# A hybrid encoder layer on one core: six 2048x2048 products as Strassen-Winograd block products, with the weights as the moving operand

## The chip, the cores and the metric

The kernel runs on one core of a Trainium2 chip. The metric is the device time of one launch in microseconds (us); lower is better. Five engines take part, each with its own queue of instructions that starts them strictly in order: TensorE (PE: matmuls and transposes; its weight loads are listed apart as PEld), VectorE (DVE), ScalarE (ACT), GpSimd (POOL) and SyncE (SP), which here only issues DMAs; ScalarE issues some too. Instructions of different engines wait for each other by semaphores.

## The reference

One layer on 512 tokens of 2048 channels, in float32:

```python
h = rmsnorm(x, norm_w)
u = h @ w_in
z_ssm, xbc, dt_f, dt_b, q_a, kv_a, z_attn, g_ssm, g_attn = jnp.split(u, cuts, axis=-1)
# branch A: depthwise conv + SiLU on xbc, bidirectional chunked SSD scan, D skip
y = y.reshape(b, s, D_SSM) * jax.nn.silu(z_ssm)
y = rmsnorm(y.reshape(b, s, SSM_GROUPS, D_SSM // SSM_GROUPS),
            ssm_norm_w.reshape(SSM_GROUPS, D_SSM // SSM_GROUPS)).reshape(b, s, D_SSM)
# branch B: low-rank q and kv with RMSNorm, rotary part, softmax attention over 16 heads: o
o = o * jax.nn.silu(z_attn)
# merge: sigmoid gates, one projection per branch, output projection, residual
m = sigmoid(g_ssm) * (y @ w_proj_ssm) + sigmoid(g_attn) * (o @ w_proj_attn)
x = x + m @ w_out
```

and a last RMSNorm over the channels. Six of the products are 512x2048 by 2048x2048: the columns of w_in for z_ssm, g_ssm and g_attn, then w_proj_ssm, w_proj_attn and w_out. The scan works in four chunks of 128 tokens and four groups of eight heads.

## The kernel before, in words

Every float32 product is made from three matmuls in a rounded format: an operand is split into a high part (a cast on ScalarE) and a low part (the difference, on VectorE), and high x high, high x low and low x high are added up in PSUM (mm3, L158 to L160). Weights are stationary (128x128), 512 tokens are moving, and results have channels on the partitions ("dims-major"). A tile is 128 output channels: 16 blocks of the 2048 inputs by 3 matmuls, 48 in all. wchunk (L148 to L154) brings half a tile's weights, 128x1024: a load into the tile wraw, the cast to wh, the difference to wl, three buffers of each.

The activations h live in SBUF as h_h and h_l. The program runs: RMSNorm and transposes; the tile of dt; four scan groups; the rest of the gate tiles, the compressed q and kv; attention head by head; w_proj_ssm, w_proj_attn, w_out; final norm.

A scan group first computes its six tiles of xbc (conv and SiLU on ScalarE and VectorE) and then does the scan, a long chain of small steps over VectorE, ScalarE and GpSimd. While that chain runs, TensorE gets other tiles as fill: the group's four z tiles and eleven gate tiles. fill.run hands out their matmuls in 18 gaps, 40 in each, at fixed places of the program. A step (one chunk, half the group's heads) holds the making of a 128x512 decay matrix G (L548 to L559), a gap, and diag (L569 to L579), which multiplies G with the inputs, transposes the skip term yo (L575), adds and multiplies by z. The tile framework sets each engine's order from the order of the program, in which loads and splits of weights are moved ahead by a number of instructions (tc.high_priority).

The same way attention has fill from the next heads and, in its last head, from w_proj_ssm. The tag st names three buffers of 128x512 that all gate results and fetches share.

## Time and profile before

| | |
|---|---|
| median of three runs | 2069.2 us (2068.72 to 2069.51) |
| profiled execution | 2069.04 us |
| its span, first to last instruction | 2067.3 us |
| PE busy | 2035.6 us, 9498 instructions |
| VectorE, ScalarE, GpSimd busy | 1122.7, 791.2, 189.8 us |
| DMA | 252.16 MB, 122 GB/s in the mean |
| granted TensorE clock, mean | 0.998 |

A row of the groups reads: line, engine, operation, output<-inputs, shapes, number of instructions, busy us, mean ns of one, idle time of that engine before them and what ended it. A row of the DMA issues reads: destination<-source, queue, count, KB each, median us from issue to landing. A row of a timeline reads: start us, duration us, engine, line, operation. A row of windows reads: stretch, its length, then for PE, PEld, DVE, ACT and POOL the busy us with the number of instructions, then granted clock (1 is full), share of the DMA engines, GB/s.

### The profile page before, as it was taken

Reading aid. Unit: us, or ns where it says so; the run is one execution under the profiler, and the core shown is the slowest. Engines: PE = TensorE matmul, PEld = TensorE weight load, DVE = VectorE, ACT = ScalarE, POOL = GpSimd, SP = SyncE. Lnnn points to the kernel's source line nnn. Section 1 sums busy time; section 2 is a strip of 40 time slices with the busy share of each in tenths; the row PEclk is TensorE's granted clock in tenths of the full one; section 3 lists DMA queues with packets and bytes.
Section 4 is the critical chain, followed back from the end, with each engine's and each line's share of the span. In section 5 each row is a group of like instructions: output and inputs, shape, how many; then the busy total and the mean of one; then the engine's idle time right before and its main releaser. Section 6 shows DMA issues by size and latency. Waiting matters only on the chain.

```text
span 2067.3 us, 24135 instructions
## 1 busy us (share of the span) xinstructions
PE 2035.6 (98%) x9498; PEld 1681.3 (81%) x9498; DVE 1122.7 (54%) x1531; ACT 791.2 (38%) x1103; POOL 189.8 (9%) x139
## 2 busy tenths in 40 slices
PE   6999999999999999999999999999999999999998
PEld 5888888888888888888788888888878888888886
DVE  4646755567545675447674657677663334343342
ACT  5433443334433354334433434444442222222232
POOL 1031000311003100111100000000011010000110
PEclk9999999999999999999999999999999999999999
DMA  5423443245332453224433333323345444335342
GB/s 186 124 82 116 155 131 112 87 128 162 121 108 83 148 153 122 92 90 150 138 122 103 105 119 88 102 81 98 102 123 168 145 150 134 122 119 182 104 141 81
DMA packets 116881, 252.16 MB, mean 122 GB/s; under 512 B 11168, under 2 KB 44064, under 8 KB 116768
## 3 DMA queue, kind: packets, MB, share of 16 engines
q1 hardware_dynamic: 101088, 222.33, 34.7%
q10 hardware_dynamic: 15680, 28.29, 3.7%
q8 instruction: 74, 1.21, 0.2%
q14 instruction: 39, 0.32, 0.0%
HBM read 220.96 MB, written 25.43 MB: 119 GB/s over the span
## 4 chain that ended last, share of the span: by engine, by line
PE 98%; DVE 1%; DMA 1%; ACT 0%; issue 0%; ACTq 0%
PE gp L158 8%; PE gp L159 8%; PE gp L160 8%; PE mm L160 6%; PE mm L158 6%; PE mm L159 6%; PE zp L158 3%; PE zp L160 3%; PE f L997 3%; PE zp L159 3%; PE f L998 3%; PE f L999 3%; PE pb L845 1%; PE qp L160 1%; PE qp L158 1%; PE qp L159 1%
## 5 line engine op out<-in xcount | busy, mean ns | idle before, releaser
L154 DVE TENSOR_TENSOR wl<-wraw,wh 128x1024 fp32r<-128x1024 f32 (+2 forms) x332 | 401.7, 1210 | 571.5 <-ACT wh L153 549.2
L153 ACT CAST wh<-wraw 128x1024 fp32r<-128x1024 f32 (+1 forms) x336 | 341.3, 1017 | 828.8 <-PE gp L159 214.1
L158 PE MATMUL gp<-h_h,wh 128*128 128x512 f32 x768 | 302.4, 394 | 0.0
L159 PE MATMUL gp<-h_l,wh 128*128 128x512 f32 x768 | 299.2, 390 | 0.0
L160 PE MATMUL gp<-h_h,wl 128*128 128x512 f32 x768 | 299.1, 390 | 0.0
L158 PE MATMUL mm<-h_h,wh 128*128 128x512 f32 x544 | 215.2, 396 | 0.0
L160 PE MATMUL mm<-h_h,wl 128*128 128x512 f32 x544 | 212.0, 390 | 0.0
L159 PE MATMUL mm<-h_l,wh 128*128 128x512 f32 x544 | 211.8, 389 | 0.0
L160 PEld LDWEIGHTS gp<-h_h,wl 128*128 128x128 f32 x768 | 144.2, 188 | 30.3
L158 PEld LDWEIGHTS gp<-h_h,wh 128*128 128x128 f32 x768 | 144.3, 188 | 29.9 <-issue 0.9
L159 PEld LDWEIGHTS gp<-h_l,wh 128*128 128x128 f32 x768 | 144.3, 188 | 29.3 <-issue 0.2
L159 PEld LDWEIGHTS mm<-h_l,wh 128*128 128x128 f32 x544 | 102.2, 188 | 22.0 <-issue 1.2
L158 PEld LDWEIGHTS mm<-h_h,wh 128*128 128x128 f32 x544 | 102.2, 188 | 21.8 <-issue 1.2
L160 PEld LDWEIGHTS mm<-h_h,wl 128*128 128x128 f32 x544 | 102.1, 188 | 21.5
L158 PE MATMUL zp<-h_h,wh 128*128 128x512 f32 x256 | 100.5, 392 | 0.0
L160 PE MATMUL zp<-h_h,wl 128*128 128x512 f32 x256 | 99.7, 389 | 0.0
L159 PE MATMUL zp<-h_l,wh 128*128 128x512 f32 x256 | 99.6, 389 | 0.0
L548 DVE TENSOR_TENSOR_SCAN sum<-da,scn 128x512 f32<-128x512 f32 x64 | 83.4, 1318 | 0.0
L997 PE MATMUL f<-wh,mh 128*128 128x512 f32 x208 | 80.9, 389 | 0.0
L998 PE MATMUL f<-wl,mh 128*128 128x512 f32 x208 | 80.9, 389 | 0.0
L999 PE MATMUL f<-wh,ml 128*128 128x512 f32 x208 | 80.9, 389 | 0.0
L835 ACT ACTIVATE pr<-s,nm 128x512 f32<-128x512 f32 x64 | 44.1, 689 | 79.7 <-DVE nm L833 78.2
(3625 smaller groups left out, 3715.0 us busy)
## 6 DMA issues: line engine op xcount, KB each, us to landing
wraw<-wi SPq DMA_DIRECT2D x198, 512.0 KB, 3.5
da<-da_d SPq DMA_DIRECT2D x64, 256.0 KB, 3.8
wraw<-wps SPq DMA_DIRECT2D x32, 512.0 KB, 3.5
wraw<-wpa SPq DMA_DIRECT2D x32, 512.0 KB, 3.7
wraw<-wo SPq DMA_DIRECT2D x32, 512.0 KB, 3.5
wraw<-wun SPq DMA_DIRECT2D x16, 384.0 KB, 3.0
xt<-x SPq DMA_DIRECT2D x8, 512.0 KB, 8.5
zs_d<-gate ACTq DMA_DIRECT2D x16, 256.0 KB, 2.9
```

Of the source, the lines that this page charges most:

```text
L153: act.copy(h, raw)
L154: (dve if ahead[0] else pool).tensor_sub(l, raw, h.bitcast(F32))
L158: pe.matmul(out, wh, xh, start=start, stop=False)
L159: pe.matmul(out, wh, xl, start=False, stop=False)
L160: pe.matmul(out, wl, xh, start=False, stop=stop)
L548: dve.tensor_tensor_scan(sums[dd], flat(da), mask, 0.0, ALU.add, ALU.mult)
L835: act.activation(pr, s, AF.Exp, bias=nm, scale=SCALE, accum_out=sm_)
L845: pe.transpose(tp[:, k * P:(k + 1) * P], prs[t][:, k * P:(k + 1) * P], ident)
L997: pe.matmul(acc, mh[:, tk], h[k], start=(kk == 0), stop=False)
L998: pe.matmul(acc, mh[:, tk], l[k], start=False, stop=False)
L999: pe.matmul(acc, ml[:, tk], h[k], start=False, stop=(kk == KT - 1))
```

## The change

**The products.** The six 2048x2048 products are taken out of the scan, of attention and of the old tail, and all run behind attention, in the order wz, wgs, wga, wps, wpa, wo, each as a stage of the class Winograd. A stage splits the weights into 2x2 blocks in each of two column pairs cp, and the activations into 2x2 blocks (inputs by tokens). Of a pair it makes seven block products P1 to P7 (Winograd's form of Strassen) instead of eight, each of 48 matmuls: 14 x 48 = 672 in a stage, before 16 x 48 = 768. Weights (128x512) are now the moving operand, and a 128x128 piece of the activations is stationary, so results have tokens on the partitions.

**Operands.** A stage needs seven activation operands: the blocks x11, x12, x22 and the sums S1 to S4. x_op makes one in two halves from pieces of 512 KB read from DRAM: pieces go into buffers of the tag wraw (three, shared with the weights), are added up by GpSimd and VectorE, cast and split. The weight combinations are made by w_sub on GpSimd from the loads called held (eight buffers); the first combination, t3, is made in a wraw buffer. The three stages with input h share their operands. Each of wps, wpa and wo gets its own, made while the stage before runs its second pair (pass_on, make); for wo, whose input m is the result of wpa, S3 and x11 are made early from what is there, S1, S2 and x22 after wpa's last result, S4 and x12 after the transposes of that last result.

**Ways through DRAM.** h is added up from h_h and h_l again after scan group 0 (16 GpSimd additions hf, L633) and written out. The scan writes y unnormed, token-major (diag no longer transposes yo); norm and gate follow behind wz (done_z). Results that feed a product (y behind wz, m behind wpa) are transposed on TensorE (turn) and written out.

**The scan's fill.** The six xbc tiles of the next group and the ten tiles of the compressed q and kv are now fill, with the gate tiles of attention (za): 10, 10, 10 and 11 tiles, 26.7 matmuls in a gap (29.3 in the last group).

The core of the diff:

```diff
+    def qkv_gen(i, sq, new):
+        p_ = mm("qkv")
+        yield from gemm_steps(p_, win(T_QKV + i), h_h, h_l)
+        g_ = st("qkv")
+        act.copy(g_, p_)
+        put(qkv_d[i], g_)
+        if i in (0, 6):
+            act.activation(sq, p_, AF.Square)
+        else:
+            s2 = new("s2")
+            act.activation(s2, p_, AF.Square)
+            dve.tensor_add(sq, sq, s2)
...
+        if g + 1 < GROUPS:
+            for i in range(6):
+                fill.add(("xbc", g + 1) if i == 5 else "xbc", xbc_gen(g + 1, i))
+        for kind, n in ((("qkv", 4),), (("qkv", 4),), (("qkv", 2), ("za", 2)), (("za", 11),))[g]:
+            add_fill(kind, n)
+        left = [(10 * 48, 10 * 48, 10 * 48, 11 * 48)[g], 18]
...
-                yt = pb("yt")
-                for ct in range(4):
-                    pe.transpose(yt[:, ct * P:(ct + 1) * P], yo[:, c, ct * P:(ct + 1) * P], ident)
-                ys_ = tmp2("ys_")
-                act.copy(ys_, yt)
-                dve.tensor_add(ys_, ys_, yb)
-                dve.tensor_mul(zs[:, :, cs], zs[:, :, cs], ys_.rearrange("p (t l) -> p t l", t=4))
+                yt = st("yt")
+                dve.tensor_add(yt, yo[:, c], yb)
+                put(y_d[c][g], yt)
...
+        if g == 0:
+            for k in range(KT):
+                hf = st("hf")
+                pool.tensor_add(hf, h_h[:, k, :].bitcast(F32), h_l[:, k, :].bitcast(F32))
+                put(k_tile(h_d, k), hf)
+        if g == 2:
+            put(rkv_d, r_sum(sq_kv, KL, tmp2))
+        if g == 1:
...
+    def x_op(which, src, place):
+        op_pool, tag, n = place
+        op = op_pool.tile([P, 2, 8, 256], F32R, tag=tag, bufs=n, name=which)
+        for q in range(2):
+            def piece(ij):
+                t = wp.tile([P, 1024], F32, tag="wraw", bufs=3, name="xraw")
+                i, j = int(ij[0]) - 1, int(ij[1]) - 1
+                s_ = src[j].rearrange("p (k t) -> p k t", k=8)[:, 4 * q:4 * q + 4, i * 256:(i + 1) * 256]
+                nc.sync.dma_start(t.rearrange("p (k t) -> p k t", k=4), s_)
+                return t
+            def add(t, u):
+                pool.tensor_add(t, t, u)
+            def sub(t, u):
+                pool.tensor_sub(t, t, u)
+            def dadd(t, u):
+                dve.tensor_add(t, t, u)
+            def dsub(t, u):
+                dve.tensor_sub(t, t, u)
+            first, *rest = {"x11": ["11"], "x12": ["12"], "x22": ["22"], "S1": ["21", (add, "22")],
+                            "S2": ["21", (add, "22"), (dsub, "11")], "S3": ["11", (sub, "21")],
+                            "S4": ["12", (dadd, "11"), (dsub, "21"), (sub, "22")]}[which]
+            t = piece(first)
+            for f, ij in rest:
+                f(t, piece(ij))
+            t = t.rearrange("p (k t) -> p k t", k=4)
+            ks = slice(4 * q, 4 * q + 4)
+            act.copy(op[:, 0, ks], t)
+            dve.tensor_sub(op[:, 1, ks], t, op[:, 0, ks].bitcast(F32))
+        return op
...
+    def w_raw(w, cp, kh, cb, m, held=False):
+        with tc.high_priority(offset=LOAD_AHEAD if held else AHEAD):
+            if held:
+                t = xb.tile([P, 1024], F32, tag="held", bufs=8, name="held")
+            else:
+                t = wp.tile([P, 1024], F32, tag="wraw", bufs=3, name="wraw")
+            nc.sync.dma_start(t, a[w][cp, kh, cb, m])
+        return t
+    def w_sub(out, x, y):
+        with tc.high_priority(offset=AHEAD):
+            pool.tensor_sub(out, x, y)
+    def w_split(raw):
+        with tc.high_priority(offset=AHEAD):
+            h = wp.tile([P, 1024], F32R, tag="wh", bufs=3, name="wh")
+            l = wp.tile([P, 1024], F32R, tag="wl", bufs=3, name="wl")
+            act.copy(h, raw)
+            dve.tensor_sub(l, raw, h.bitcast(F32))
         return h, l
...
+    def rows(bank, op, i, m, w):
+        h, l = w
+        for jj in range(2):
+            j = 2 * m + jj
+            xh, xl = (op[:, s, j, i * P:(i + 1) * P] for s in range(2))
+            wh, wl = (t[:, jj * 512:(jj + 1) * 512] for t in (h, l))
+            pe.matmul(bank, xh, wh, start=(j == 0), stop=False)
+            pe.matmul(bank, xh, wl, start=False, stop=False)
+            pe.matmul(bank, xl, wh, start=False, stop=(j == 7))
+    def product(where, name, op, chunk):
+        banks = [b(name) for b in BANKS[where][name]]
+        for m in range(4):
+            w = w_split(chunk(m))
+            for i in range(2):
+                rows(banks[i], op, i, m, w)
+            yield 12
+        product_done()
+        yield banks
...
+        def t1(self, cp, m):
+            b11 = w_raw(self.w, cp, 0, 0, m)
+            w_sub(self.t[m], self.t[m], b11)
+            return b11
+        def t3(self, cp, m):
+            self.hold(cp, m)
+            t3 = wp.tile([P, 1024], F32, tag="wraw", bufs=3, name="t3")
+            w_sub(t3, self.b22[m], self.t[m])
+            return t3
...
+                yield from steps(product("head", "P7", self.op("S3"), lambda m: self.t3(0, m)), got)
+                self.p7 = evict(got.pop())
+                self.make(*ORDER)
+                yield from steps(product("head", "P1", self.op("x11"), lambda m: self.t1(0, m)), got)
...
+        def pair(self, cp):
+            w, got = self.w, []
+            end = cp == 1
+            if not end:
+                p7, p1 = self.p7, self.p1
+            else:
+                p1 = self.p1b
+                self.b22, self.t = [], []
+                def c7(m):
+                    t3 = self.t3(1, m)
+                    self.t1(1, m)
+                    return t3
+                yield from steps(product(1, "P7", self.op("S3"), c7), got)
+                p7 = evict(got.pop())
+                self.used("S3", "x11")
+            b22, t = self.b22, self.t
+            yield from steps(product(cp, "P5", self.op("S1"), lambda m: t[m]), got)
+            p5 = got.pop()
+            if end:
+                self.used("S1")
+                if self.nxt:
+                    self.nxt.make("S3", "x11")
+            def c6(m):
+                w_sub(t[m], b22[m], t[m])
+                return t[m]
+            yield from steps(product(cp, "P6", self.op("S2"), c6), got)
+            if end:
+                self.used("S2")
+                self.pass_on("S1")
+            p6 = got.pop()
+            us, vs_ = [], []
+            for i in range(2):
+                u = kp_.tile([P, SEQ], F32, tag="kk", bufs=2, name="u")
+                dve.tensor_add(u, p1[i], p6[i])
+                v = p7[i]
+                dve.tensor_add(v, v, u)
+                o22 = st("o22")
+                dve.tensor_add(o22, v, p5[i])
+                dve.tensor_add(u, u, p5[i])
+                us.append(u)
+                vs_.append(v)
+                self.done(2 + i, 2 * cp + 1, o22)
+            yield from steps(product(cp, "P3", self.op("S4"), lambda m: b22[m]), got)
+            if end:
+                self.used("S4")
+                self.pass_on("S2")
+            p3 = got.pop()
+            for i in range(2):
+                dve.tensor_add(us[i], us[i], p3[i])
+                self.done(i, 2 * cp + 1, us[i])
+            b21 = []
+            def c4(m):
+                b21.append(w_raw(w, cp, 1, 0, m, True))
+                w_sub(t[m], b21[m], t[m])
+                return t[m]
+            yield from steps(product(cp, "P4", self.op("x22"), c4), got)
+            if end:
+                self.used("x22")
+                self.pass_on("S4")
+            p4 = got.pop()
+            for i in range(2):
+                dve.tensor_add(vs_[i], vs_[i], p4[i])
+                self.done(2 + i, 2 * cp, vs_[i])
+            if end and self.w == "wo":
+                yield from self.last_product(p1, b21)
+                return
+            yield from steps(product(cp, "P2", self.op("x12"), lambda m: b21[m]), got)
+            if end:
+                self.used("x12")
+                self.pass_on("x22", "x12")
+                if self.nxt:
+                    self.nxt.make("S1", "S2", "x22")
+            p2 = got.pop()
+            for i in range(2):
+                dve.tensor_add(p1[i], p1[i], p2[i])
+                self.done(i, 2 * cp, p1[i])
...
+        def pass_on(self, *which):
+            if self.nxt and self.w != "wpa":
+                self.nxt.make(*which)
...
+    def turn(tile_, t, b, dst, n):
+        def f():
+            tp = pb("turn")
+            for i in range(4):
+                pe.transpose(tp[:, i * P:(i + 1) * P], tile_[:, i * P:(i + 1) * P], ident)
+            o = st("turned")
+            act.copy(o, tp)
+            d = dst[b // 2].rearrange("p (k t) -> p k t", k=8)[:, 4 * (b % 2):4 * (b % 2) + 4, t * P:(t + 1) * P]
+            act.dma_start(d, o.rearrange("p (k t) -> p k t", k=4))
+        after(n, f)
...
+    def done_z(t, b, z):
+        act.activation(z, z, AF.Silu)
+        y = fetch(y_d[t][b], "y")
+        dve.tensor_mul(z, z, y)
+        s_ = ssz[:, 4 * t + b:4 * t + b + 1]
+        act.activation(y, z, AF.Square, accum_out=s_)
+        dve.tensor_scalar(s_, s_, 1.0 / 512, EPS, ALU.mult, ALU.add)
+        r = rsqrt1(s_)
+        w = fetch(a["snw"][:, b * 512:(b + 1) * 512].broadcast_to([P, SEQ]), "snw")
+        dve.scalar_tensor_tensor(z, z, r, w, ALU.mult, ALU.mult)
+        turn(z, t, b, yn_d, 2)
...
+    def done_pa(t, b, o):
+        g_ = fetch(ga_d[t][b], "ga")
+        dve.tensor_mul(o, o, g_)
+        m_ = fetch(ms_d[t][b], "ms")
+        dve.tensor_add(o, o, m_)
+        turn(o, t, b, m_d, 1)
...
+    stages = [("wz", h_d, done_z), ("wgs", h_d, done_gate(gs_d)), ("wga", h_d, done_gate(ga_d)),
+              ("wps", yn_d, done_ps), ("wpa", o_d, done_pa), ("wo", m_d, done_o)]
+    prods = [Winograd(*s_) for s_ in stages]
+    for p_, q_ in zip(prods, prods[1:]):
+        if q_.src is p_.src:
+            q_.ops = p_.ops
+        else:
+            p_.nxt = q_
```

How the order moves, at three places. GpSimd, from the last decay matrices of scan group 0 into group 1 (G is the backward half of the decay matrix, c_l a split, yo the skip term and its sums, xw the weighted inputs from which the chunk states, loc, are made). Before:

```order
L557 TENSOR_TENSOR G_2036<-dtT,cbb 128x512
L557 TENSOR_TENSOR G_2124<-dtT,cbb 128x512
L447 TENSOR_TENSOR c_l<-CT,c_h 128x512
L483 TENSOR_TENSOR xw<-xT,wst 128x512 x2
L516 TENSOR_TENSOR yo<-xT,dsk 128x512 x4
```

Now:

```order
L599 TENSOR_TENSOR G_1904<-dtT,cbb 128x512
L633 TENSOR_TENSOR hf<-h_h,h_l 128x512 x13
L558 TENSOR_TENSOR yo<-xT,dsk 128x512
L633 TENSOR_TENSOR hf<-h_h,h_l 128x512
L558 TENSOR_TENSOR yo<-xT,dsk 128x512
L633 TENSOR_TENSOR hf<-h_h,h_l 128x512
L558 TENSOR_TENSOR yo<-xT,dsk 128x512 x2
L633 TENSOR_TENSOR hf<-h_h,h_l 128x512
L525 TENSOR_TENSOR xw<-xT,wst 128x512 x4
```

The sixteen hf stand between group 0's last G and group 1's first xw.

GpSimd, at the start of wz behind attention (held_9360, 9367, 9374 and 9381 take the weight combinations of the four chunks; xraw_9387 and 9394 become the two halves of S1, which P5 needs). Before, GpSimd had, towards the end of attention, only splits of y:

```order
L867 TENSOR_TENSOR y0l<-y0st,y0h 128x512
L867 TENSOR_TENSOR y2l<-y2st,y2h 128x512
L867 TENSOR_TENSOR y4l<-y4st,y4h 128x512
L867 TENSOR_TENSOR y6l<-y6st,y6h 128x512
L867 TENSOR_TENSOR y8l<-y8st,y8h 128x512
```

Now:

```order
L930 TENSOR_TENSOR held_9360<-held_9360,wraw_9362 128x1024
L930 TENSOR_TENSOR held_9367<-held_9367,wraw_9369 128x1024
L930 TENSOR_TENSOR held_9360<-held_9358,held_9360 128x1024
L930 TENSOR_TENSOR held_9374<-held_9374,wraw_9376 128x1024
L930 TENSOR_TENSOR held_9367<-held_9365,held_9367 128x1024
L930 TENSOR_TENSOR held_9374<-held_9372,held_9374 128x1024
L930 TENSOR_TENSOR held_9381<-held_9381,wraw_9383 128x1024
L884 TENSOR_TENSOR xraw_9387<-xraw_9387,xraw_9389 128x1024
L884 TENSOR_TENSOR xraw_9394<-xraw_9394,xraw_9396 128x1024
```

Seven weight subtractions stand ahead of the two additions of S1; three of them already belong to P6. On SP's queue, held_9381 stands ahead of the pieces of S1.

GpSimd, from the last product of wpa into wo (held_15021 to 15096 are weights of wpa's P4; xraw_15610 and 15617 become S1 of wo, 15625 and 15635 S2, 15779 and 15792 S4; t3 are the weights of P7). Before, GpSimd had no instruction between the last split of o and the tail. Now:

```order
L930 TENSOR_TENSOR held_15071<-held_15459,held_15071 128x1024
L930 TENSOR_TENSOR held_15096<-held_15478,held_15096 128x1024
L884 TENSOR_TENSOR xraw_15610<-xraw_15610,xraw_15612 128x1024
L884 TENSOR_TENSOR xraw_15617<-xraw_15617,xraw_15619 128x1024
L884 TENSOR_TENSOR xraw_15625<-xraw_15625,xraw_15627 128x1024
L884 TENSOR_TENSOR xraw_15635<-xraw_15635,xraw_15637 128x1024
L930 TENSOR_TENSOR t3_15674<-held_15670,held_15672 128x1024
L930 TENSOR_TENSOR t3_15696<-held_15692,held_15694 128x1024
L930 TENSOR_TENSOR t3_15718<-held_15714,held_15716 128x1024
L930 TENSOR_TENSOR t3_15740<-held_15736,held_15738 128x1024
L887 TENSOR_TENSOR xraw_15779<-xraw_15779,xraw_15787 128x1024
L887 TENSOR_TENSOR xraw_15792<-xraw_15792,xraw_15800 128x1024
```

S1 and S2 stand ahead of t3, S4 ahead of the weights of the second product. On SP's queue the pieces of S4 and x12 stand in the same way ahead of wraw_15816, the first weights of P1.

517 lines of the change are left out of this document (249 added, 268 removed).

## The prediction

> **What bounds the kernel now.** I read the page first: busy shares, slices, chain.
>
> ```profile
> span 2067.3 us, 24135 instructions
> PE 2035.6 (98%) x9498; PEld 1681.3 (81%) x9498; DVE 1122.7 (54%) x1531; ACT 791.2 (38%) x1103; POOL 189.8 (9%) x139
> PE   6999999999999999999999999999999999999998
> DVE  4646755567545675447674657677663334343342
> PE 98%; DVE 1%; DMA 1%; ACT 0%; issue 0%; ACTq 0%
> ```
>
> TensorE is busy in nearly every slice, and the chain that ended last is 98% TensorE work. VectorE has half its time free, GpSimd nine tenths. So removed matmuls pay in full, as long as nothing else becomes late; every microsecond in which TensorE waits is lost.
>
> Matmul records overlap (390 ns each), so their price is their distance, from the timeline of TensorE in the first projection, which runs at full clock:
>
> ```profile
> 1699.69 0.39 PE L159 MATMUL ps__13311<-y1l,wh 128*128 128x512 f32 x1
> ...
> 1702.41 0.39 PE L159 MATMUL ps__13311<-y5l,wh 128*128 128x512 f32 x1
> ```
>
> Twelve steps in 2.72 us: 0.2267 us a matmul, 10.88 us for a tile or block product of 48.
>
> **Prices of everything else**, from the groups by form, the DMA issues and the life of the tile wraw:
>
> ```profile
> L154 DVE TENSOR_TENSOR wl<-wraw,wh 128x1024 fp32r<-128x1024 f32 x292 | 367.8, 1260 | 556.3 <-ACT wh L153 535.2 <-PE rp L318 16.8 <-PE pb L298 4.2
> L153 ACT CAST wh<-wraw 128x1024 fp32r<-128x1024 f32 x296 | 311.2, 1052 | 787.2 <-PE gp L159 209.3 <-PE mm L159 178.0 <-PE f L999 68.9
> L154 POOL TENSOR_TENSOR wl<-wraw,wh 128x1024 fp32r<-128x1024 f32 x4 | 9.5, 2389 | 32.0 <-ACT wh L153 32.0
> L512 POOL TENSOR_TENSOR yo<-yo,tmp 128x512 f32<-128x512 f32 x24 | 36.9, 1552 | 184.3 <-DVE tmp L511 184.3
> L575 PE MATMUL yt<-cst,yo 128*128 128x128 f32 x64 | 10.5, 287 | 0.0
> wraw<-wps SPq DMA_DIRECT2D x32, 512.0 KB, 3.5
> y_d<-yn ACTq DMA_DIRECT2D x16, 256.0 KB, 2.0
> o_d<-og ACTq DMA_DIRECT2D x16, 256.0 KB, 3.7
> zs_d<-gate ACTq DMA_DIRECT2D x16, 256.0 KB, 2.9
> L150 SPq DMA_DIRECT2D wraw<-wps x32: 327/332/510, 1477.0 to 1680.9; - x32
> DMA to landing us min/median/max: 2.5/3.5/9.8
> ```
>
> On 128x1024, a VectorE subtraction is 1.26 us, a ScalarE cast 1.05, a GpSimd addition 2.39 (four operations only, the weakest row here); a GpSimd addition on 128x512 is 1.55; a 512 KB load lands in 3.5, a 256 KB store in 2.0 to 3.7. The new operand pieces have 1 KB runs instead of 4 KB, which no row shows; between 2.5 (the shortest landing) and 9.8 I take the median, since the size is that of the weight chunks. SP issues a load in 0.33 us; it gets about 800 instead of 574, and at most some forty fall into the 65 us around a change of stage: its rate is no limit, only what stands waiting at its head.
>
> **The saving.** Six products go from 16x48 to 14x48 matmuls: 6x96 = 576 x 0.2267 = 130.6 us. Transposes: the chain shows
>
> ```profile
> 315.51 0.44 PE pb L424 x4
> ```
>
> 0.11 us each. 128 new ones for the turns of z and m are 14 us; 64 of yt go, at 10.5 us of record, about 8. Net **-124.5 us**. The other edits on TensorE are a microsecond or two: fewer r_sum matmuls, diag's token-major form with the same count. After the last matmul both kernels add, square, scale and store, and I count no difference. The first three products fill the last heads of attention as projection tiles did before, by the same matmuls, so I count nothing there either; their operands S3 and x11 are requested a head earlier, and if they came late it would be some 10 us, within the range of wz.
>
> **hf.** In group 0's end GpSimd gets 16 additions of 1.55 us, through three st buffers, each emptied by a ScalarE-queue store of about 2.9 us; four yo stand between and behind them, and group 1's xw come last (order above). 20x1.55 = 31 us, then xw and its splits: loc can start about 35 us after group 0's end. TensorE has some 15 us of turns and fill in the gaps before it needs them. Its fill is bound to gaps in program order, so it cannot go on with the next. Stall 20 (10 to 22; the low end if the first additions run under group 0's last steps).
>
> **Scan.** One chunk (two steps) of group 1 before, and a conv operation ahead of it:
>
> ```profile
> 465.10:486.40 21.30, 21.30 (x108) 17.08 (x110) 16.44 (x20) 9.74 (x11) 2.42 (x2) 1.00 0.51 164
> ...
> 362.52 0.74 DVE L387 SCALAR_TENSOR_TENSOR cacc<-mm,vec,cacc 128x510 f32<-128x510 f32 x1
> ```
>
> TensorE is full, VectorE has 16.44 of 21.3. A step's gap held 40 fill matmuls, now 26.7: TensorE 10.65 - 13.3x0.2267 = 7.6, and 7.3 without the yt turns. VectorE: 8.22, less 0.56 wl of 1.26, less half a product of 0.68 (z is no longer multiplied here), plus for half a tile of xbc three conv operations of 0.74, or one addition of 0.68 where the tile is qkv: 7.5 to 8.3. So VectorE becomes the limit, by a few tenths where the fill is qkv or za and by 1 us where it is xbc, whose 288 matmuls a group are gone after 10.8 of the 18 gaps: about 8 us over 32 steps. The two r_sum chains that now stand at the ends of groups 1 and 2 (six VectorE operations of 0.68 and a square root, before the next group's work on the same queue) add 5 each: 18 (5 to 40, the high end if all 32 steps lose 1 us). Before attention, the compressed and rotary parts (some 35 to 43 us of VectorE by the same prices) stand beside three za tiles, 32.6 us: 4 (0 to 10).
>
> **Start of wz.** The load of held_9381 waits for the last head's store out of the memory that it takes over, and holds SP's queue; on GpSimd its subtraction, the last of seven, stands ahead of S1's addition (order above). From the last pv: 0.9 for its product, 3.7 for the store, 3.5 for the load, two GpSimd operations 4.8, cast 1.05: P5 starts at 14 to 16, where P1b has ended at 3.2. S2 then comes 1 and 3 us late with its two halves and S4 5 and 6, since a half of S4 is load, addition, a fourth load into a buffer just freed, addition, subtraction, cast, split (3.5+1.26+3.5+2.39+1.05+1.26 with one addition under the load). 12 + 4 + 11, and 7 for the fetches of done_z on the same SP queue (16 of y and 16 of the gain, through three st buffers): **34** (20 to 45).
>
> **wga to wps, wps to wpa.** 26 pieces pass three wraw buffers. In series, with the next half's first piece already landed: S3 14 us, x11 4, S1 12, S2 17, S4 24, x22 4, 75 in all. Cover from P5's end: P6, P3, P4, P2, 43.5 us, plus at most P5's own 10.9. S4 and x22 stand ahead of t3 on SP and GpSimd, so P7 waits for nearly all. 25 each, **50** (2x8 to 2x31).
>
> **wpa to wo.** No cover, since m is finished by wpa's last product. From its last matmul: turns, copy, store 5.2; SP issues a piece at 5.5; landing 9.3; S1 takes two GpSimd additions (to 11.7, 17.6) with reloads between; S2 from 17.6 to 34.3 (two reloads of 3.5, two additions, two splits); t3's buffer is S2's last: 36.7, cast and split 39. P7 starts at **38** instead of 0. After P7 the last turn again: S4 (24 us), its last buffer takes wraw of P1 (3.5, cast, split): **35** more. Together 73 (55 to 85; each of some dozen landings at 2.5, the shortest in the trace, would take 12 off).
>
> **VectorE and GpSimd side by side.** In the scan:
>
> ```profile
> 447.98 2.02 POOL L557 TENSOR_TENSOR G<-dtT,cbb 128x512 f32<-128x512 f32 x1
> 447.03 2.06 DVE L154 TENSOR_TENSOR wl<-wraw,wh 128x1024 fp32r<-128x1024 f32 x1
> 449.02 1.52 DVE L558 TENSOR_TENSOR G<-G,G 128x512 f32<-128x512 f32 x1
> 454.50 0.68 DVE L558 TENSOR_TENSOR G<-G,G 128x512 f32<-128x512 f32 x1
> ```
>
> The same product takes 0.68 alone and 1.52 beside a GpSimd operation, wl 2.06. GpSimd goes from 190 to about 745 us by these prices (32 weight subtractions and 8 operand additions a stage). In the steady stages wgs and wga: GpSimd 32x2.39 = 76, VectorE 56x1.26 + 13 = 83, ScalarE about 75, all under TensorE's 152, and weights wait three deep, so no stall there. In the four stages that make operands the chains above stretch: **32** in all (0 to 60).
>
> **Clock after stalls.** At the end of attention:
>
> ```profile
> 1520.00:1525.00 5.00, 4.11 (x16) 3.45 (x17) 3.92 (x10) 3.41 (x8) 1.27 (x1) 0.71 0.46 140
> 1520.89 0.63 PE L845 MATMUL pb<-cst,pr 128*128 128x128 f32 x4 [2.52 <-DVE nm L833]
> ...
> 1522.90 1.05 PE L845 MATMUL pb<-cst,pr 128*128 128x128 f32 x4
> ...
> 1525.69 0.40 PE L158 MATMUL op<-pt_h,v_h 128*128 128x512 f32 x1
> ```
>
> After a wait of 2.5 us the granted clock is 0.71; the four transposes and five matmuls from 1522.90 take 2.8 us instead of 4x0.11 + 5x0.2267 = 1.6, and those before them lose another 0.4. About 1.6 us lost a stall, some ten stalls: 15 (8 to 20).
>
> **Sum.** 20 + 18 + 4 + 34 + 50 + 73 + 32 + 15 = 246, less 124.5: +121.5. The profiled execution took 2069.04 us (1.74 outside its span), the runs' median is 2069.2, the same within 0.2%, which is about what a measurement here can tell from no change. 2069.0 + 121.5 = **2190 us**. All low ends give 10+5+0+20+16+55+0+8 = 114, so 2059; all high ends 344, so 2289.
>
> **Rivals.** (a) *The loads come early enough.* Operands S3, x11, S1, S2 of a stage may be requested as soon as the older stage's operand falls free; if the piece chains run under P5 to P2 and the scan is still held by TensorE, only what has no cover stays: the low ends of the terms, 2059. It decides as soon as all stalls together stay under 124.5. For it:
>
> ```profile
> q1 hardware_dynamic: 101088, 222.33, 34.7%
> q10 hardware_dynamic: 15680, 28.29, 3.7%
> ```
>
> the DMA engines are 38% busy, and a landing may be 2.5. Against it: 73 of the 124.5 is gone in one transition by a chain that no early request shortens. Chance 0.16.
>
> (b) *VectorE and GpSimd exclude each other*: only one of two-input operations runs at a time. A stage with operands then needs 40x2.39 + 76x1.26 + about 26 short ones of 0.68 = 209 us against 152: 57 lost in each of four, 228, in place of the 189 that the terms from wz to the stretching hold: 2230; above the four, chains and exclusion add up, so to 2290. For it: the four rows above. Against: operations that read PSUM or one input may be free of it, and low stretch in windows with few GpSimd operations. Chance 0.22. The Trainium skill says so for this pair ("SBUF — State Buffer", Who interferes with whom: a two-input VectorE instruction and a GpSimd instruction that reads SBUF share one port pair, whichever starts first keeps it to its end); the four rows agree with it, and by it alone (b) would be the likeliest.
>
> (c) *The saving isn't all there*: not likely, as the weights' 128x512 moving form is the same as before; 0.03 that everything cancels within 0.2%.
>
> **How the numbers follow.** The forecast 0.59, with its own range 2090 to 2245; (b) 0.22; (a) 0.16; no difference 0.03. So faster 0.16, same 0.03, slower 0.81. 8 in 10: from 2065, which leaves (a) out, to 2270.
>
> **What would show it.** TensorE's busy share at 85 to 90%, its slices full to the end of attention except for one gap at 20 us after group 0, then gaps at four places: before P5 of wz, before P7 of wps and of wpa, two before P7 and P1 of wo, the last two 30 us or more each, with releasers xraw loads and GpSimd. wgs and wga at 152 us each without gaps. A VectorE split far over 1.26 us in the mean speaks for (b). I am wrong if the two gaps of wo are short, or if wgs and wga are longer than 160.

## The result: 17% slower

The changed kernel takes 2428.6 us in the median (2425.2 to 2431.5), the kernel before 2069.1: a ratio of 1.174 (95% interval 1.172 to 1.176). The forecast was slower, 2190; the loss is three times what it gave, and the time lies far outside the range.

The page of the kernel after, its head, slices and chain:

```profile
span 2429.7 us, 24971 instructions
PE 2026.8 (83%) x8978; PEld 1643.8 (68%) x8978; DVE 1738.9 (72%) x1943; ACT 988.1 (41%) x1327; POOL 815.4 (34%) x365
PE   6999798999999999985778999984986496733976
PEclk9999899999999999997899999997998798866988
PE 48%; DVE 20%; DMA 15%; POOL 7%; issue 6%; ACT 3%; SPq 0%; ACTq 0%; POOLq 0%; DVEq 0%
```

TensorE lost its place: 48% of the chain instead of 98%. The books close on two numbers. TensorE's idle time rose from 2067.3 - 2035.6 = 31.7 us to 2429.7 - 2026.8 = 402.9, by 371. Its busy time fell by 8.8 us only, though 124.5 us of work was taken out, so what is left costs 116 us more. Most of it is the clock, whose granted mean fell from 0.998 to 0.922. By the clock records of the trace it stood at half in 39 stretches, which hold 169 us of TensorE's busy time; at 0.43 us a step instead of 0.23 some 80 us of that are lost. About 20 more come of the waits themselves: the last matmul before a wait counts with its whole 0.39 us instead of a step of 0.23, and there are 134 waits (of more than 0.06 us) against 8 before. The other 16 stay open. 371 - 9 = 362, the whole difference of the spans.

What TensorE waited for from the first product on (line, releaser, us in all, times, longest), in the kernel after:

```profile
PE P L955 <- ACT wh L936: 149.1, 15, 39.9
PE P L956 <- DVE wl L937: 89.8, 59, 7.6
PE P L955 <- ACT S L903: 35.1, 5, 20.7
PE turn L1173 <- DVE o L1215: 26.2, 4, 10.0
PE turn L1173 <- DVE p L1215: 9.0, 4, 3.9
```

Fifteen waits for the high part of weights, up to 39.9 us long, are mostly the gaps at the changes of stage. Beside them stand 59 waits of 1.5 us in the mean for the low part of weights, all over the stages, and waits of transposes; neither was in the forecast.

From the starts of the products in the trace, the stages last (dense: 14 x 10.88 = 152.3 us):

| stage | after | e1_dve_sums | e2_no_combos | e3_one_set | e6_dve_spread |
|---|---|---|---|---|---|
| start of wz's first product | 1068 | 1062 | 1069 | 1068 | 1063 |
| wz (from there, with attention's end) | 252 | 227 | 213 | 251 | 230 |
| wgs | 173 | 157 | 160 | 172 | 158 |
| wga | 210 | 190 | 162 | 159 | 166 |
| wps | 227 | 199 | 177 | 170 | 192 |
| wpa | 252 | 224 | 202 | 208 | 207 |
| wo | 231 | 211 | 225 | 189 | 202 |

Two engines in each other's way. Groups by form, of the kernel after and, below, of the kernel of the first experiment, in which VectorE does GpSimd's sums:

```profile
L937 DVE TENSOR_TENSOR wl<-held,wh 128x1024 fp32r<-128x1024 f32 x236 | 405.8, 1732 | 101.6 <-ACT wh L936 96.8 <-issue 2.7 <-DMA ga_d<-u 0.9
L930 POOL TENSOR_TENSOR held<-held 128x1024 f32<-128x1024 f32 x96 | 268.0, 2800 | 239.4 <-DVE wl L937 89.9 <-DVE u L1094 30.8 <-DMA held<-wgs 22.6
L1096 DVE TENSOR_TENSOR p<-p,u 128x512 f32<-128x512 f32 x24 | 44.1, 1837 | 0.0
L1094 DVE TENSOR_TENSOR u<-p,P 128x512 f32<-128x512 f32 x24 | 15.4, 680 | 0.0
```

```profile
L937 DVE TENSOR_TENSOR wl<-held,wh 128x1024 fp32r<-128x1024 f32 x236 | 288.3, 1226 | 77.1 <-ACT wh L936 75.9
L930 DVE TENSOR_TENSOR held<-held 128x1024 f32<-128x1024 f32 x96 | 117.4, 1232 | 0.9
L1096 DVE TENSOR_TENSOR p<-p,u 128x512 f32<-128x512 f32 x24 | 16.4, 685 | 0.0
L1094 DVE TENSOR_TENSOR u<-p,P 128x512 f32<-128x512 f32 x24 | 15.5, 681 | 0.0
```

The same subtraction wl takes 1.73 us beside GpSimd's sums and 1.23 without them; the addition p<-p,u 1.84 and 0.69. The addition u<-p,P, which reads one input from PSUM (P), takes 0.68 in both. The trace of the kernel after says the same by itself: of the 332 splits wl of its products, the 159 that overlap a GpSimd operation by more than 0.1 us take 2.37 us in the mean and the other 173 take 1.22, while of the 72 additions with one input in PSUM 48 overlap one and take 0.68 like the rest. All in all the 815 instructions that VectorE has in both kernels from the first product on take 1012 us in the kernel after and 713 in the other.

In a steady part of wgs one sees single operations collide (start, duration; VectorE, then GpSimd):

```profile
1465.76 1.22 DVE L937 TENSOR_TENSOR wl<-held,wh 128x1024 fp32r<-128x1024 f32 x1
1468.81 4.08 DVE L937 TENSOR_TENSOR wl<-held,wh 128x1024 fp32r<-128x1024 f32 x2
1483.96 3.28 DVE L937 TENSOR_TENSOR wl<-held,wh 128x1024 fp32r<-128x1024 f32 x1
...
1468.26 2.40 POOL L930 TENSOR_TENSOR held<-held 128x1024 f32<-128x1024 f32 x1 [4.71 <-DMA held<-wgs]
1483.76 2.40 POOL L930 TENSOR_TENSOR t<-held 128x1024 f32<-128x1024 f32 x1 [3.13 <-DMA held<-wga]
```

A split that meets a GpSimd subtraction lasts 1.2 us plus most of the 2.4 of the other: 3.28 from 1483.96, against 1.22 at 1465.76. The Trainium skill ("SBUF — State Buffer", Who interferes with whom) has a VectorE instruction with two SBUF inputs and a GpSimd instruction that reads SBUF exclude each other for the whole of the one that came first; these rows agree.

And what a short wait costs, TensorE's timeline at the start of wps:

```profile
1703.13 0.79 PE L955 MATMUL P<-wh,S 128*128 128x512 f32 x1 [25.43 <-ACT wh L936]
...
1705.83 0.63 PE L956 MATMUL P<-wl,S 128*128 128x512 f32 x1
1706.26 0.63 PE L957 MATMUL P<-wh,S 128*128 128x512 f32 x1
...
1708.57 0.40 PE L957 MATMUL P<-wh,S 128*128 128x512 f32 x1
1708.80 0.40 PE L955 MATMUL P<-wh,S 128*128 128x512 f32 x1
1711.00 0.49 PE L956 MATMUL P<-wl,S 128*128 128x512 f32 x1 [1.81 <-DVE wl L937]
...
1712.32 0.63 PE L957 MATMUL P<-wh,S 128*128 128x512 f32 x1
1712.75 0.63 PE L955 MATMUL P<-wh,S 128*128 128x512 f32 x1
...
1715.21 0.40 PE L955 MATMUL P<-wh,S 128*128 128x512 f32 x1
```

After the wait of 25 us steps are 0.43 apart until 1708, then 0.23. The next wait, of 1.8 us, brings 0.43 again, from 1711.6 to 1714.9: eleven steps from 1711.00 to 1715.21 take 4.2 us instead of 2.5. So this wait of 1.8 us cost 1.7 us more in slow steps, not much less than the wait of 25 (some 2.2).

Not every short wait does that. From the first product on TensorE has 101 waits of more than 0.06 us. Of the 59 under 1.5 us, 10 are followed within 3.5 us by a stretch at half clock or lie in one; of the 11 between 1.5 and 2 us, 7; of the 31 longer ones, 29. Before each of the 28 stretches that begin among the products, TensorE had been idle for at least 1.76 us of the last 3.41 (the length of the shortest stretch).

### The profile page after: what moved, and what is told of

Same layout as the page of the kernel before. It is cut to its first block, busy times and chain, and to the rows that moved or that the text cites. A ratio compares the mean times of both kernels' runs of the same rounds, so it can differ in the third digit from the quotient of the medians.

```text
span 2429.7 us, 24971 instructions
## 1 busy us (share of the span) xinstructions
PE 2026.8 (83%) x8978; PEld 1643.8 (68%) x8978; DVE 1738.9 (72%) x1943; ACT 988.1 (41%) x1327; POOL 815.4 (34%) x365
## 4 chain that ended last, share of the span: by engine, by line
PE 48%; DVE 20%; DMA 15%; POOL 7%; issue 6%; ACT 3%; SPq 0%; ACTq 0%; POOLq 0%; DVEq 0%
DVE wl L937 6%; PE P L956 4%; PE P L957 4%; PE P L955 4%; PE za L166 2%; PE za L164 2%; PE za L165 2%; POOL held L930 2%; DMA xraw<-yn_d 2%; DMA xraw<-m_d 2%; PE xbc L164 2%; PE xbc L165 2%; PE xbc L166 2%; DVE sum L590 1%; POOL xraw L887 1%
## 5 line engine op out<-in xcount | busy, mean ns | idle before, releaser
L937 DVE TENSOR_TENSOR wl<-held,wh 128x1024 fp32r<-128x1024 f32 x236 | 405.8, 1732 | 101.6 <-ACT wh L936 96.8
L955 PE MATMUL P<-wh,S 128*128 128x512 f32 x768 | 316.5, 412 | 148.6 <-ACT wh L936 113.4
L936 ACT CAST wh<-held 128x1024 fp32r<-128x1024 f32 x236 | 246.1, 1050 | 303.5 <-PE P L957 191.3
L956 PE MATMUL P<-wl,S 128*128 128x512 f32 x768 | 318.4, 415 | 41.0 <-DVE wl L937 39.0
L930 POOL TENSOR_TENSOR held<-held 128x1024 f32<-128x1024 f32 x96 | 268.0, 2800 | 239.4 <-DVE wl L937 89.9
L957 PE MATMUL P<-wh,S 128*128 128x512 f32 x768 | 312.9, 407 | 5.4 <-DVE small L1194 3.3
L955 PEld LDWEIGHTS P<-wh,S 128*128 128x128 f32 x768 | 153.0, 199 | 188.6 <-ACT wh L936 118.6
L160 DVE TENSOR_TENSOR wl<-wraw,wh 128x1024 fp32r<-128x1024 f32 (+2 forms) x146 | 172.8, 1184 | 130.0 <-ACT wh L159 123.9
L956 PE MATMUL P<-wl,x 128*128 128x512 f32 x464 | 192.6, 415 | 51.1 <-DVE wl L937 50.8
L955 PE MATMUL P<-wh,x 128*128 128x512 f32 x464 | 189.8, 409 | 35.7 <-ACT wh L936 35.7
L956 PEld LDWEIGHTS P<-wl,S 128*128 128x128 f32 x768 | 152.7, 199 | 90.5 <-DVE wl L937 57.1
L957 PE MATMUL P<-wh,x 128*128 128x512 f32 x464 | 188.3, 406 | 1.2 <-DVE small L1194 1.2
L957 PEld LDWEIGHTS P<-wh,S 128*128 128x128 f32 x768 | 152.5, 199 | 39.4 <-DVE S L904 4.1
```

What stands on the lines that cost most here:

```text
L160: (dve if ahead[0] else pool).tensor_sub(l, raw, h.bitcast(F32))
L930: pool.tensor_sub(out, x, y)
L936: act.copy(h, raw)
L937: dve.tensor_sub(l, raw, h.bitcast(F32))
L955: pe.matmul(bank, xh, wh, start=(j == 0), stop=False)
L956: pe.matmul(bank, xh, wl, start=False, stop=False)
```

## The experiments

Theories at the start. L, the prediction's: the chains of operand loads and sums at the changes of stage are the loss. X, its rival (b): GpSimd's sums and VectorE's two-input work exclude each other everywhere, and the short waits that come of it pull the clock down. A time without an interval is a single run; the kernel e8_hf_early gave 2212, and 2219 to 2228 when it was timed again, so single runs less than some 15 us apart are not told apart.

**All sums on VectorE.**

```diff
 def add(t, u):
-    pool.tensor_add(t, t, u)
+    dve.tensor_add(t, t, u)
 def sub(t, u):
-    pool.tensor_sub(t, t, u)
+    dve.tensor_sub(t, t, u)
 def w_sub(out, x, y):
-        pool.tensor_sub(out, x, y)
+        dve.tensor_sub(out, x, y)
```

> All weight combinations and operand sums of the products go from GpSimd to VectorE (32 subtractions and 8 additions a stage, 1.26 us instead of 2.39 to 2.8). Theory X (GpSimd and VectorE keep each other out on two-input operations, and the many short waits for weight splits that follow let the clock drop): the mean of the split wl falls from 1.73 to about 1.26 us, the stages without operands of their own (wgs: 83 + 32x1.26 = 123 us of VectorE) run at 152 us, and the time falls to 2200 to 2290. Theory L (the operand chains in series through three buffers are the loss, as the prediction has it): only the chain's GpSimd steps get shorter, some 8 a stage by 1.2 us, four stages: about 2390.

2282.0 us, 147 less than the kernel after. VectorE does some 224 operations more, and yet is less busy:

```profile
span 2280.2 us, 24727 instructions
PE 1984.8 (87%) x8978; PEld 1627.0 (71%) x8978; DVE 1690.0 (74%) x2167; ACT 992.0 (44%) x1327; POOL 200.8 (9%) x141
```

1690 us instead of 1739. wl's mean is 1.23 us, the waits of TensorE for it fall from 59 (89.8 us) to 22 (25.7 us), and wgs is at 157 us, where X gave 152. The time lies in X's range, and L's 2390 is out. The 147 us hold two things that this run does not part: VectorE is no longer held up, and a sum takes 1.23 us instead of 2.4 to 2.9. Of the 150 us of span, 107.5 are idle time of TensorE (402.9 to 295.4) and 42 faster steps (2026.8 to 1984.8). The big gaps before the first products stay where they were, 27, 31, 42 and 37 us long: they are the part that L is about.

**No weight combinations.**

```diff
 def w_sub(out, x, y):
-        pool.tensor_sub(out, x, y)
+        pass
 ...
-    t3 = wp.tile([P, 1024], F32, tag="wraw", bufs=3, name="t3")
-    w_sub(t3, self.b22[m], self.t[m])
-    return t3
+    return self.b22[m]
```

> The weight combinations are left out (the raw weight blocks are multiplied, so the results are not the layer's); loads, splits, operands and matmuls stay. GpSimd keeps 8 additions a stage. X: split at 1.26 us, wgs at 152 us, 2130 to 2230 in all. L: the loss at the changes of stage stays, and only t3's place behind the operands goes: 2350 to 2400.

2227.6 us, 201 less, at the upper end of what X gave. The stages keep 160 to 225 us: what is left beside the combinations is the operands, the turns and the norm behind wz, which this run does not part. In wo the two gaps of 43 and 40 us become one of 58 before P1: P7, whose weights are no longer made behind the operands, starts at once, and P1 waits for the pieces that stand ahead of its weights.

**One set of operands for all stages.**

```diff
-    if q_.src is p_.src:
-        q_.ops = p_.ops
-    else:
-        p_.nxt = q_
+    q_.ops = p_.ops
```

> All six stages use the operands of h (so the last three products multiply the wrong activations); the operand making of wps, wpa and wo with its 84 loads is left out. L: every stage behind wz comes down to 152 us, and the time to about 2430 - 21 - 57 - 75 - 100 - 70 = 2110. X: these stages come down only to wgs's 173 us, splits stay at 1.6 us or more: about 2200.

2236.2 us, 192 less; wl stays at 1.76 us in the mean. The later stages come down to 159 to 208 us, not to 152: neither number was met, and the result lies nearer X's. wpa's 208 us without any operand to make showed a third loss. Twice there, P3 lasts some 25 us, because the transposes of the results stand in TensorE's queue and wait for a fetch (ms), whose issue stands on SP's queue behind a weight load, which in its turn waits for VectorE's splits. The same place in the kernel after, from its chain of waits:

```profile
2005.30 2.28 DVE wl L937 x2
...
2007.60 0.33 SPq L925
...
2007.97 0.02 SPq L1165
...
2008.02 6.06 DMA ms<-ms_d
...
2014.17 2.25 DVE o L1215
2016.42 0.14 issue
2016.56 1.09 PE turn L1173 x4
```

**Leaving out hf.**

```diff
-                hf = st("hf")
-                pool.tensor_add(hf, h_h[:, k, :].bitcast(F32), h_l[:, k, :].bitcast(F32))
-                put(k_tile(h_d, k), hf)
+                put(k_tile(h_d, k), h_h[:, k, :].bitcast(F32))
```

> The 16 GpSimd additions that rebuild h are left out; the high part alone is written out (three products lose the low part of their input). The prediction's term: 20 us less, 2409. If the scan's other work on VectorE takes its place: within 5 us of 2429.

2410.2 us, 18 less; all of it before the products (the first starts at 1052 instead of 1068). The term of 20 holds.

**Operands requested behind the first products.** S4, x22 and x12, and for wo S1 and S2 too, are made behind P7, P1 and P1b of the stage that needs them, one behind each of the first two and the rest behind P1b:

```diff
         if end:
             self.used("x22")
-            self.pass_on("S4")
 ...
-            self.pass_on("x22", "x12")
-            if self.nxt:
-                self.nxt.make("S1", "S2", "x22")
 ...
     self.p7 = evict(got.pop())
-    self.make(*ORDER)
+    self.make(*self.todo[:1])
     ... P1 ...
     self.p1 = evict(got.pop())
+    self.make(*self.todo[:1])
     ... P1b ...
     self.p1b = evict(got.pop())
+    self.make(*ORDER)
```

> Only the place of the operand making changes: S4, x22, x12 of wps and wpa and all of S1, S2, x22, S4, x12 of wo are requested one by one behind the next stage's first products (P7, P1, P1b) instead of ahead of them. Sums stay on GpSimd. Theory L (the first product of a stage waits behind a chain of operand pieces that it doesn't need): the waits of 38, 42, 54 and 40 us before P7 of wps, wpa, wo and P1 of wo fall to under 15 each, about 110 to 130 us less: 2300 to 2320. Rival D (the pieces, the weights and the results together fill the DMA engines there, so the wait only moves to a later product): 2380 to 2430.

2379.3 us: 49 less, where L's account of the order gave 110 to 130; the time is D's lower end. The gaps before P7 of wps, wpa and wo are gone (P2 lasts 11, 14 and 17 us instead of 38, 42 and 54), and more than half comes back one product later: P7 28, 32 and 23 us, P1 of wo 30.

**Both edits together.**

> As e1_dve_sums (all sums on VectorE) with the operand making spread out as in e5_spread. If exclusion and order are separate causes their gains add up: 2282 less 110 to 130: 2150 to 2175. If VectorE, which now carries everything, is the limit where operands are made: 2220 or more.

2231.0 us: 51 less than e1_dve_sums. The time is in the second range, but that does not show VectorE as the limit: with the sums on GpSimd the order gave 49 us, so the two causes add up at the size that e5_spread had found. Why the order gave only half shows at the change from wga to wps in e1_dve_sums, in its chain of waits:

```profile
1601.79 6.55 DMA xraw<-yn_d
1608.37 1.24 DVE xraw L890
1609.62 4.65 DMA xraw<-yn_d
1614.37 1.24 DVE xraw L887
1615.62 4.55 DMA xraw<-yn_d
1620.27 1.24 DVE xraw L890
1621.52 3.58 DMA xraw<-yn_d
1625.19 1.24 DVE xraw L887
1626.44 1.05 ACT S L903
```

This is S4 as the prediction described it: load, sum, load, sum through buffers just freed. But the windows ahead of it show the DMA engines filling up (the last two columns, their busy share and GB/s):

```profile
1554.00:1565.00 11.00, 11.00 (x50) 9.13 (x49) 9.46 (x9) 6.96 (x7) 0.00 (x0) 1.00 0.64 184
1565.00:1580.00 15.00, 11.72 (x51) 9.00 (x49) 13.47 (x15) 5.68 (x6) 0.00 (x0) 1.00 0.90 291
1580.00:1596.70 16.70, 14.22 (x49) 11.20 (x50) 15.12 (x16) 7.78 (x9) 0.00 (x0) 0.80 0.79 257
1596.70:1607.00 10.30, 10.14 (x44) 7.71 (x43) 7.59 (x7) 4.20 (x5) 0.00 (x0) 1.00 1.00 333
```

The next stage's held weights come at the same time as the pieces, and these land in 6.55 us at first and 3.58 at last, where the prediction took 3.5. VectorE too is busy for 86 to 91% of the first three windows and 74% of the last (the third busy time). That a transfer put later pays only half fits with both; no run tells them apart.

**The operand sums back on GpSimd.** As e6_dve_spread, with only w_sub on VectorE:

> As e6_dve_spread, but the eight operand sums of a stage stay on GpSimd; only the 32 weight combinations go to VectorE. By exclusion a sum on GpSimd costs VectorE more (2.4 us in which its two-input work waits) than doing it there (1.23 us): 10 to 30 us slower than e6_dve_spread. If VectorE's load is the limit: faster than it.

2265.2 us, 34 more than e6_dve_spread. Eight GpSimd sums in each of four stages, 32 of some 2.7 us, cost 34 us, a little more than forecast, though GpSimd is otherwise free in the stages. How much of this is the exclusion is not parted: VectorE's other instructions take 24 us longer (1673.9 us busy, against 1688.8 less 32 sums of 1.22), and 27 of the 34 us are lost in wo and wps, where a sum that takes twice as long also makes the chain longer.

**hf ahead of the scan.** As e6_dve_spread, with the loop over hf behind dt_make, ahead of group 0's scan:

> As e6_dve_spread, and the 16 additions hf are made ahead of scan group 0, while TensorE computes its xbc tiles, instead of between groups 0 and 1. Expected 15 to 18 us less than e6_dve_spread, the size that leaving them out had; if GpSimd then holds up conv and splits of group 0, less than 10.

2212.1 us, 19 less; the first product starts at 1056 instead of 1063. Its repetition, together with a later experiment:

> The kernel e8_hf_early again, timed in the same rounds as e13_yb_bank: 2212 us, within 5 us of the first look, 6.7 to 7.1% slower than before.

2220.6 us (2219.2 to 2227.8), 1.074 (1.072 to 1.076) of before: 8 above the first run, so hf's place is worth 10 to 19 us.

**Four more on e8_hf_early.** Held weight loads 80 instructions ahead instead of 160 (LOAD_AHEAD = 80):

> e8_hf_early with the held weight loads moved ahead by 80 instructions instead of 160. If the burst of weight loads at the changes of stage is what makes pieces land in 5 to 10 us instead of 3.5: 2180 to 2200. If the weights are needed that early: 2220 or more.

2222.5 us, and each stage within 2.0 us of its length: no effect. But the edit did not do what it was meant to. Counted from wz's third product, 138 of the 144 held loads start within 4 us of where they started in e8_hf_early, so the burst was not thinned out, and what it costs stays open.

The norm part of done_z left out:

```diff
     act.activation(z, z, AF.Silu)
-    y = fetch(y_d[t][b], "y")
-    dve.tensor_mul(z, z, y)
     ...
-    dve.scalar_tensor_tensor(z, z, r, w, ALU.mult, ALU.mult)
     turn(z, t, b, yn_d, 2)
```

> e8_hf_early without the norm part of done_z (no fetch of y and of the gain, no product with y, no norm; silu and turns stay, so the layer's y is wrong). The prediction counted 7 us for it. If the turns that wait for it, and the fetches among the operand pieces, hold wz's products back: 25 to 40 us less than 2212; else 2205.

2201.7 us, 10 to 19 less: between the two numbers. The stage itself says more than the whole time: wz with attention's end takes 206.5 instead of 229.0 us, 22 less, where the prediction counted 7; the part ahead of the products was 7 us longer in this run.

The conv with one neighbour tap of three (the lines with w(1) and w(3) left out):

> e8_hf_early with one of the three neighbour taps of the conv instead of three (xbc is wrong): 48 VectorE operations of 0.75 us, 36 us, less, 27 of them in the scan's fill. If VectorE sets the scan's pace: 15 to 27 us less than 2212. If TensorE does: 5 us or less.

2209.2 us, 3 less than the first run and 11 less than the repetition; the products start 9 and 12 us earlier than in these. That is less than the 15 to 27 of the one theory and more than the 5 of the other: VectorE's amount of work is at most a part of what holds the scan.

Operands from their first piece alone (`for f, ij in rest: f(t, piece(ij))` left out):

> e8_hf_early with every operand made of its first piece alone (sums left out, the results are wrong): 14 loads a set instead of 28, and 14 VectorE sums of 1.23 us less. If the operand chains (load, sum, load, sum) are what is left at the four changes: 90 to 130 us less, 2080 to 2120. If it is the weights' loads and VectorE's load: 70 us less at most, the sums' own time, 2140 or more.

2136.9 us, 75 to 84 less, between the two forecasts; wz, wps, wpa and wo lose 16 to 20 each. The 56 sums are 69 us of VectorE by themselves, so this doesn't tell the chain from VectorE's load. It shows how much all sums and 56 loads are worth together, and that 68 us above the kernel before remain without them.

**A second bank for yb.** In the scan, TensorE waits for the PSUM bank of yb, in e8_again (first row) as in the first trace; e13_yb_bank has no such row, and its largest are the second and third:

```diff
-    ybs[c] = pc("yb")
+    ybs[c] = pa("yb")
```

```profile
PE yb L615 <- DVE yt L618: 12.0, 7, 2.7
```

```profile
PE pb L455 <- ACT xs L411: 6.5, 1, 6.5
PE za L166 <- DVE wl L160: 5.9, 2, 4.1
```

> e8_hf_early with yb in the two buffers that hold loc and off before the steps, instead of the one that it shares with the sums of r_sum. If the wait of diag for the one bank (until VectorE has added yb to yo) is what the scan loses: 10 to 20 us less than e8_again, the clock after those waits included. If the wait moves to the next link of the step's chain: within 4 us of it.

2208.7 us (2203.0 to 2213.9), 12 less than e8_again in the same rounds. diag cannot start a chunk before VectorE has read the last chunk's sums out of the one bank; before, with 40 fill matmuls in the gap, TensorE had no wait at all there.

**Turns a product later.** As e13_yb_bank, with turn(..., yn_d, 3) and, for m's second and fourth column blocks (`b % 2`), turn(..., m_d, 2):

> e13_yb_bank with the turns of y a product later (three instead of two behind their result) and those of m's second column block a product later (two instead of one). If the 30 us that the turns wait there cost time of their own: 20 to 35 us less than e13_yb_bank's 2209. If the results are held longer and the three st buffers, which they occupy, hold up the fetches instead: within 8 us of it, or slower.

2203.6 us (2191.7 to 2207.7), 5 less, with overlapping ranges: no difference is shown. The waits of the turns fell from 30 to 23 us and have another releaser (ScalarE's copy of the turn before), so they mostly moved. This is the fastest form that still computes the layer: 1.065 (1.063 to 1.067) of the kernel before. No form beat the kernel before.

## Why the prediction was wrong

It had the sign, and most of the places; two of its terms were a fraction of what they are, and one wait was missing. Two of its own signs of being wrong came up: wgs and wga take 173 and 210 us instead of 152, and the split wl 1.73 us in the mean.

- **Saving, 124.5.** Holds where nothing waits: the first eight products of wga stand 10.9 us apart, but for two of 12.2 and 12.4.
- **hf, 20.** 18 measured by leaving it out (single runs).
- **Scan, 18 + 4.** From 100 to 700 us TensorE is idle for 33 us, hf's part among them, and its mean clock is 0.96: some 55 in all against 42 with hf. But the mechanism was another: less VectorE's sum of work (one tap instead of three, 27 us less in the fill, gave 3 to 11) than links of the step's chain that the shorter gap no longer hides, 12 of them the one bank of yb.
- **wga to wps, wps to wpa (25 each), wpa to wo (38 and 35).** The gaps are 27, 31, 43 and 40 us long, at the places and with the chains that the prediction named. For wpa to wo the working holds. For the first two the match is in part luck: from the end of P5 to the next stage's P7 the prediction has 43.5 + 25 = 68 us, the trace 87 and 92, and the gap itself stayed small because P6, P3 and P4, which cover the chain, were longer too (some 17, 13 and 20 us instead of 10.9). What e5_spread added: requested later, the chains still cost more than half of it, in another place.
- **Start of wz, 34.** From P5 to the end of its stage wz takes 187 us against 120, 68 more, and P5 comes some 20 late: 88. The fetches and the norm of done_z are 22 instead of 7 (measured in e8_hf_early), and with the sums on VectorE wz loses 26 less. The rest of the 88 is not parted.
- **"VectorE and GpSimd side by side", 32: this step failed.** The prediction had the rows (wl 2.06, the product 1.52 beside GpSimd), and priced them as a stretch of the operand chains alone, in the four stages that make operands; for wgs and wga it compared busy sums with TensorE's 152 us and concluded "no stall there". In its place: VectorE's two-input work on SBUF and GpSimd's sums exclude each other in every stage, which stretched the same VectorE instructions from 713 to 1012 us, and moving the sums alone gave 147 us. wgs took 173 us, and 157 without them. That the one engine's busy time of 76 us and the other's of 83 are each under 152 says little when the one's 2.4 us come as a delay into the other's 1.26. Why three buffers of weights did not cover that delay is argued here, not tested.
- **"Clock after stalls", 15: this step was mis-sized.** The price of 1.6 us each was near, the count was not. It counted some ten long stalls; the trace has 39 stretches at half clock, and some 80 us lost in them, about 2 us each. Ten of them lie ahead of the products; before 15 of the other 29 stands a wait of only 2 to 4 us, for weights, operands or turns. About 20 us more, the ends of matmuls before waits, were not priced.
- **Not priced: the turns.** What stands in TensorE's queue behind results that still need two fetches waits with them: 38 us in the kernel after (the rows above and one of 2.9 from done_z). What these waits cost is not shown, since in e14_turn_later 7 of 30 us of them went and no difference in time is shown.
- **After the last matmul, 0.** From the end of the last product to the end of the span the kernel after takes 15.9 us, the kernel before 9.3.

Rival (b) named the mechanism with 22% and gave 2230 to 2290; it was right in kind and too small as well. It counted the exclusion in the four stages with operands alone, where wgs lost 21 us too, and it kept the 15 us for the clock.

What stays open: how much of the rest (135 us in e14_turn_later above the kernel before, 260 above the dense sum) is DMA bandwidth, VectorE's load or the three buffers. More buffers were not tried.

## What to carry to other kernels

A kernel whose TensorE is 98% of the chain seems to have the other engines to spare. Yet this form, which saves 6% of TensorE's work (124.5 of 2069 us) and nearly doubles the busy time of VectorE and GpSimd together (from 1313 to 2554 us, 1891 with all sums on VectorE), gives back more than it saved: twice in the best form here, nearly four times in the first. Count GpSimd's sums as time taken from VectorE's two-input work, not as free engine time: here VectorE's own 1.23 us was the cheaper price. And look at TensorE's waits one by one, with the clock that follows them: here most waits over 2 us were followed by a stretch at half clock, some 2 us dear, and most under 1.5 us were not.

## What the runs showed of the hardware

- A wait of TensorE of 1.8 us could be enough to halve the pace of its matmuls (0.43 instead of 0.23 us) for 3.3 us; of 11 waits between 1.5 and 2 us 7 were followed by half clock or lay in it, of 59 shorter ones 10.
- Beside GpSimd's sums VectorE's subtraction of two SBUF operands took 2.37 us instead of 1.22; its addition with one operand in PSUM took 0.68 us either way.
- With GpSimd's sums gone (e1_dve_sums) VectorE did 224 more instructions in 49 us less busy time; its 128x1024 subtraction went from 1.73 to 1.23 us in the mean.
- At a change of stage of e1_dve_sums the DMA engines ran full at 333 GB/s, and a 512 KB piece on the chain landed in 6.55 us.
